# A two-layer decoder trunk on one core: key products among the index scores, all of the forgetting half ahead of the other half, and three weight splits moved from GpSimd to VectorE

## The chip, the core and the metric

The kernel runs on one core of a Trainium2 chip. The metric is the device time of one execution in microseconds (us). TensorE multiplies, VectorE (DVE in the rows), ScalarE (ACT) and GpSimd (POOL) do the elementwise work, SyncE (SP) and the other engines issue the DMAs. PEld is TensorE's weight load.

## The reference, cut to what matters

```
x: (1, 512, 1024) float32, two layers
even layer: h = x @ w_in, split into q_a, c_kv, q_idx, k_idx, w_idx, q_b, k_b, v_b, f_in
  index scores   score[t,s] = sum over 8 heads of w_idx[t,h] * relu(q_idx[t,h] . k_idx[s]), causal
  selection      the 128 best keys of each position
  8 heads "a"    softmax over the selected keys of (q_lat . c_kv + rel_bias), values c_kv
  8 heads "b"    forgetting heads: softmax of (q_b . k_b + cum_f[t] - cum_f[s]), values v_b
  m = concat(o_a, o_b) @ w_o
odd layer : gated projections and a short causal convolution, concat, @ w_o
each layer: x = LN(alpha*x + m); x = LN(alpha*x + conv_ffn(x)),  d_ff = 2816
```

## The kernel before, in words

All products are made at a precision near float32: every operand is cut into a high and a low part, and `mm3` (lines 179 to 183) or `mms` (line 185, the same as a generator that stops after each product) makes three products of 512 columns for one. The weights come as a stream of 128 x 1024 units (`Stream`). SyncE loads a unit into one of three `raw` buffers (line 62), ScalarE copies it to the high part (line 78), and the low part is a subtraction, on VectorE (line 82) or, for the units listed in `POOL_CUT`, on GpSimd (line 80). The parts lie in `whi`/`wlo` (three buffers each) or, for units named in `ws.big`, in one of 13 `quad` buffers. `unit()` hands out the next unit and splits two units ahead.

The order in which each engine takes its instructions is made when the kernel is built: a planner goes through the program, takes on each engine the earliest instruction of the program that its own time model holds to be ready, and lets later ones fill gaps. An engine then runs its list strictly in order. PSUM has eight banks; `bank()` takes one of the five of pool `ps5`, or, while `more` is not empty, in turn of eight also one of the three of pool `ps3`. Until the attention ends, the other three banks belong to `tri`, the tile into which `turn` transposes the soft-max weights.

The even layer goes in this order. (1) The first projections. (2) `pair_b(0)` makes the queries of forgetting heads 0 and 1, 24 products and a cut. (3) `scores(j)` for the three later blocks of 128 positions: for each of 8 heads two products into a bank (line 478), a ReLU on ScalarE (line 480), and a weighted sum into `sel[j]` on VectorE (lines 483 and 485). The first block needs no selection. (4) The rest of `pair_b(0)`: 24 key products. (5) Four value projections `proj_t` of 24 products, with the rounds of the selection `choose` (lines 497 and 499) on VectorE tied behind them in fixed portions by `step`. When a block's selection is done, GpSimd rescales it (line 503). (6) `pair_b(1)`, then the loop over head pairs by the string `SEQ`: `bias` on GpSimd, `logits` on TensorE, `soft` on VectorE and ScalarE (lines 667 and 669), `turn` (line 686), `values`, `divide`. Between these, `fill` takes products from `work()` (the projections of the later heads), and when these are gone from `begin()`, which is the first half (k = 0 to 3, the forgetting heads; units 23 to 26) of the attention's output projection. While `tri` lives, `begin()` opens three of its eight banks.

(7) `out_ln` adds the second half (k = 4 to 7, units 27 to 30, `us`) and normalises, in four chunks of 128 positions. With `begun` it takes on the remaining forgetting products bank by bank: ahead of chunk n those up to chunk n + 1. Behind each chunk stands `ln_chunk`: sums and statistics on VectorE (lines 261 to 269), a power on GpSimd (266), a scaling on ScalarE (272), an addition on GpSimd (273). `ln_turn` transposes the result on TensorE (284) and cuts it (`cut2`, lines 232 and 233). The next projection needs the turned chunks. The feed-forward layers and the odd layer call the same `out_ln` without `begun`: there a head part for all chunks comes first and 24 products for each chunk after it.

(8) Behind the first layer's feed-forward block the odd layer begins with four units of v, numbers 97 to 100 of the stream. Units 97 to 99 are the three that `POOL_CUT` names besides 12 to 22. Unit 105 gets a mask on GpSimd when it has been loaded (line 832).

Of the kernel before, what the change touches and what calls it, by code (L numbers as in the profile page):

```python
# [13 lines left out]
PSUM = bass.MemoryType.PSUM  # L14
# [4 lines left out]
NCH = 4  # L19
# [8 lines left out]
TAIL = 4  # L28
SEQ = "L0 4 S0 T0 B0 L1 4 S1 V1 3 L2 2 S2 T1 B1 R0 R1 4 V0 D 3"
GROUPS = ((3,), (2, 0), (1,))  # L30
POOL_CUT = tuple(range(12, 23)) + (97, 98, 99)
S1, S2, S3, S4 = 4, 3, 1, 2
WARM, WARM2 = 7, 5

# [62 lines left out]
def _body(ctx, tc, A):  # L97
# [9 lines left out]

    ps5 = E(tc.tile_pool(name="ps5", bufs=5, space=PSUM))
    ps3 = ExitStack()
    tri = ps3.enter_context(tc.tile_pool(name="tri", bufs=1, space=PSUM))  # L110
    more = []
    turnus = [0]

    def bank():
        turnus[0] += 1
        pool = more[0] if more and turnus[0] % 8 >= 5 else ps5
        return pool.tile([128, 512], F32, name="bank")

    def temp():
        return tmp.tile([128, 512], F32, name="temp")  # L120

    def quad(dt=FR):
        return quads.tile([128, 4, 512], dt, name="quad")

    ws = Stream(nc, A["ws"], rawp, wp, 2)
    ws.on_pool = POOL_CUT
    base = [0]

    def unit():
        i = base[0]  # L130
        base[0] += 1
        return ws.get(i)
# [46 lines left out]
    def mm3(out, a, b, first, last):  # L179

        nc.tensor.matmul(out, a[0], b[0], start=first, stop=False)  # L181
        nc.tensor.matmul(out, a[0], b[1], start=False, stop=False)  # L182
        return nc.tensor.matmul(out, a[1], b[0], start=False, stop=last)  # L183
# [18 lines left out]
    def wk(w, a, b):  # L202
        return w[0][:, a:b], w[1][:, a:b]
# [6 lines left out]
    def proj(w, xt):  # L210
        p = bank()
        half(w, xt, p, 0, S)
        return p
# [26 lines left out]
    def load_gb(l, i):  # L240
        q = quad(F32)
        for s, src in enumerate((A["ln_g"], A["ln_b"])):
            nc.gpsimd.dma_start(q[:, 2 * s:2 * s + 2].rearrange("p a b -> p (a b)"),
                                src[l, i].partition_broadcast(128))
        return [q[:, j] for j in range(4)]

    def load_res(src, n):
        r = []
        for hf in range(2):
            t = temp()  # L250
            nc.gpsimd.dma_start(t, src[n * 128:n * 128 + 128, hf * 512:hf * 512 + 512])  # L251
            r.append(t)
        return r

    def ln_chunk(n, ph, res, gb, dst):
        st = sm.tile([128, 2, 6], F32, name="st")
        mv = sm.tile([128, 2], F32, name="mv")
        ve = sm.tile([128, 1], F32, name="ve")
        rs = sm.tile([128, 1], F32, name="rs")
        for hf in range(2):  # L260
            nc.vector.scalar_tensor_tensor(out=res[hf], in0=res[hf], scalar=ALPHA, in1=ph[hf],
                                           op0=ALU.mult, op1=ALU.add)
            nc.vector.bn_stats(st[:, hf], res[hf])
        nc.vector.bn_aggr(mv, st)
        nc.vector.tensor_scalar(ve, mv[:, 1:2], EPS, None, op0=ALU.add)
        nc.gpsimd.tensor_tensor(out=rs, in0=ve, in1=mhalf, op=ALU.pow)
        for hf in range(2):
            r = res[hf]
            nc.vector.scalar_tensor_tensor(out=r, in0=r, scalar=mv[:, 0:1], in1=gb[hf],  # L269
                                           op0=ALU.subtract, op1=ALU.mult)  # L270
            if n < NCH - 1:
                nc.scalar.mul(r, r, rs)
                nc.gpsimd.tensor_tensor(out=r, in0=r, in1=gb[2 + hf], op=ALU.add)
            else:
                nc.vector.scalar_tensor_tensor(out=r, in0=r, scalar=rs, in1=gb[2 + hf],  # L275
                                               op0=ALU.mult, op1=ALU.add)
            nc.sync.dma_start(dst[n * 128:n * 128 + 128, hf * 512:hf * 512 + 512], r)

    def ln_turn(n, res, xt, after):
        for hf in range(2):  # L280
            r = res[hf]
            p = bank()
            for j in range(4):
                t = nc.tensor.transpose(p[:, j * 128:j * 128 + 128], r[:, j * 128:j * 128 + 128], ident)
                if j == 0 and after is not None:
                    tc.add_manual_dep(t.ins, after.ins.name, AFTER, reason="behind the products that hide the norm")
            c = slice(n * 128, n * 128 + 128)
            cut2(xt[0][hf][:, :, c], xt[1][hf][:, :, c], p.rearrange("p (a b) -> p a b", a=4))

    def out_ln(lhs, nk, res_src, l, i, dst, nbig, last=False, begun=None):  # L290

        head = nk - TAIL
        if begun is None:
            pb = [[None, None] for _ in range(NCH)]
            for hf in range(2):
                for n in range(NCH):
                    pb[n][hf] = bank()
            for k in range(head, nk + (0 if last else nbig)):
                ws.big[base[0] + k] = quad

            for k in range(head):
                w = unit()
                for hf in range(2):
                    for n in range(NCH):
                        mm3(pb[n][hf], lhs(k, n), wk(w, hf * 512, hf * 512 + 512), k == 0, False)
        else:
            pb, run = begun
        us = [unit() for _ in range(TAIL)]
        gb = load_gb(l, i)
        xt = None if last else [[quad(), quad()], [quad(), quad()]]  # L310
        rs = []
        for n in range(NCH):
            rs.append(load_res(res_src, n))
            while begun is not None and pb[min(n + 1, NCH - 1)][1] is None and next(run, "end") != "end":
                pass
            for hf in range(2):
                for k in range(head, nk):
                    m = mm3(pb[n][hf], lhs(k, n), wk(us[k - head], hf * 512, hf * 512 + 512),
                            k == 0, k == nk - 1)
                if not last and hf == 0 and n >= 2:  # L320
                    ln_turn(n - 2, rs[n - 2], xt, m)
            ln_chunk(n, pb[n], rs[n], gb, dst)
            if not last:
                ws.ready(base[0] + n + 1)
        late = None if last else [lambda m, n=n: ln_turn(n, rs[n], xt, m) for n in (2, 3)]
        return xt, late
# [54 lines left out]
    with ExitStack() as m0:  # L381
# [90 lines left out]
        def scores(j):  # L472
            n = 128 * (j + 1)
            for h in range(NH):
                c = slice(j * 128, j * 128 + 128)
                p = bank()
                for s in range(2):
                    nc.tensor.matmul(p[:, :n], qi[h % 2][:, h // 2, c], misc[:, s, :n], start=s == 0, stop=s == 1)
                t = temp()
                nc.scalar.activation(t[:, :n], p[:, :n], AF.Relu)  # L480
                s = wi[:, j, h:h + 1]
                if h == 0:
                    nc.vector.tensor_scalar(sel[j], t[:, :n], s, None, op0=ALU.mult)
                else:
                    nc.vector.scalar_tensor_tensor(out=sel[j], in0=t[:, :n], scalar=s, in1=sel[j],
                                                   op0=ALU.mult, op1=ALU.add)
            nc.gpsimd.affine_select(out=sel[j][:, n - 128:], in_=sel[j][:, n - 128:], pattern=[[-1, 128]],
                                    compare_op=ALU.is_ge, fill=-3e38, base=0, channel_multiplier=1)
# [25 lines left out]
        def pair_b(i):  # L514
            q = made[i] = quad()
            if i >= 1:
                ws.big[base[0] + 3] = quad
            for s, scale in ((0, -float(HD ** -0.5)), (2, 1.0)):
                w = unit()
                p = bank()  # L520
                for _ in proj_steps(w, xq, p):
                    yield
                cut2(q[:, s], q[:, s + 1], p, scale)
                if i < 2:
                    step(S2)
                yield
            finished.add(i)

        pair0 = pair_b(0)
        for _ in range(25):  # L530
            next(pair0)
        for j in (1, 2, 3):
            scores(j)
# [97 lines left out]
        def bias(h):  # L631
            if h < 16:
                biases[h] = (bias_b if h < 8 else bias_a)(h % 8)
# [113 lines left out]
        def lhs(k, n):  # L747
            c = slice(n * 128, n * 128 + 128)
            return oq[k // 2][:, k % 2, c], oq[k // 2][:, 2 + k % 2, c]

        pb = [[None, None] for _ in range(NCH)]
# [13 lines left out]
        begun = begin()  # L765
# [7 lines left out]
        def fill(n):  # L773
            for _ in range(n):
                next(todo, None)

        bias(0)
        bias(1)
        for i in range(10):
# [40 lines left out]
    with ExitStack() as m1:  # L820
# [59 lines left out]
        for i in range(4):  # L880
# [15 lines left out]
            pb = proj(unit(), xt)  # L896
# [97 lines left out]
```

## Time and profile before

| | |
|---|---|
| median of 3 runs | 1188.36 us (1187.03 to 1191.15) |
| the profiled execution's own time | 1188.65 us |
| its span, first to last instruction | 1186.9 us |
| mean granted TensorE clock | 0.992 of full speed |

The profile is of one execution. Its span is 1.75 us shorter than its own time; the execution lies 0.29 us above the median. A granted clock of 1.00 is 2.4 GHz, 0.50 is 1.2 GHz.

### The profile page before, as it was taken

What the parts mean: (1) busy time and instruction counts of PE and PEld (TensorE: products, weight loads), DVE (VectorE), ACT (ScalarE), POOL (GpSimd) and SP (SyncE); (2) the same over time, 40 slices, a digit from 0 to 9 for tenths busy, and PEclk for the clock granted to TensorE, in tenths of its full rate; (3) what the DMA queues carried; (4) which work ended last, traced back from release to release, by engine and by line L of the source; (5) the groups of instructions that cost most, each with busy time, mean ns of one, the idle gap of its engine ahead of it and who ended that gap; (6) DMA issues with size and microseconds to landing.
All of it is one profiled execution on the core that took longest, in us unless ns stands there. A gap on an engine that the chain in (4) does not pass through costs nothing. (4 is left out here: it accounts for less than half of the span.)

```text
span 1186.9 us, 14468 instructions
## 1 busy us (share of the span) xinstructions
PE 1157.8 (98%) x5532; PEld 960.0 (81%) x5532; DVE 692.9 (58%) x1134; ACT 464.0 (39%) x701; POOL 193.0 (16%) x251
## 2 busy tenths in 40 slices
PE   9899999899999999999999899999999999999997
PEld 7687877778888888888887688888888888888885
DVE  6788886557655666552227754456655666552226
ACT  7515657533444443432133232332444443432121
POOL 1218647214000000010014300003000000010003
PEclk9999999899999999999999899999999999999999
DMA  7522213343232323343245123371232323344221
GB/s 253 189 71 86 76 37 89 97 162 125 72 107 89 107 89 101 112 142 107 90 167 169 46 90 129 125 241 74 71 106 90 104 92 96 117 143 142 89 89 71
DMA packets 42261, 132.03 MB, mean 111 GB/s; under 512 B 5560, under 2 KB 6656, under 8 KB 42192
## 3 DMA queue, kind: packets, MB, share of 16 engines
q1 hardware_dynamic: 37280, 116.41, 29.9%
q0 software_dynamic: 4784, 14.67, 3.8%
q8 instruction: 43, 0.70, 0.3%
q14 instruction: 26, 0.21, 0.1%
q10 hardware_dynamic: 128, 0.03, 0.0%
HBM read 122.63 MB, written 10.02 MB: 112 GB/s over the span
## 5 line engine op out<-in xcount | busy, mean ns | idle before, releaser
L82 DVE TENSOR_TENSOR wlo<-raw,whi 128x1024 fp32r<-128x1024 f32 x150 | 186.1, 1242 | 281.4 <-ACT whi L78 281.2
L181 PE MATMUL bank<-quad,whi 128*128 128x512 f32 (+2 forms) x860 | 325.3, 379 | 1.4 <-ACT whi L146 0.8
L183 PE MATMUL bank<-quad,wlo 128*128 128x512 f32 (+2 forms) x860 | 325.4, 378 | 0.0
L182 PE MATMUL bank<-quad,whi 128*128 128x512 f32 (+2 forms) x860 | 325.4, 378 | 0.0
L78 ACT CAST whi<-raw 128x1024 fp32r<-128x1024 f32 x158 | 166.3, 1053 | 263.0 <-PE bank L183 119.8
L181 PEld LDWEIGHTS bank<-quad,whi 128*128 128x128 f32 x860 | 161.5, 188 | 31.5 <-ACT whi L146 1.3
L183 PEld LDWEIGHTS bank<-quad,wlo 128*128 128x128 f32 x860 | 161.7, 188 | 29.6
L182 PEld LDWEIGHTS bank<-quad,whi 128*128 128x128 f32 x860 | 161.8, 188 | 29.4 <-DVE quad L154 0.2
L182 PE MATMUL bank<-wlo,quad 128*128 128x512 f32 x356 | 138.5, 389 | 0.0
L183 PE MATMUL bank<-whi,quad 128*128 128x512 f32 x356 | 138.3, 389 | 0.0
L181 PE MATMUL bank<-whi,quad 128*128 128x512 f32 x356 | 138.2, 389 | 0.0
L251 POOL DMA_DIRECT2D temp<-x x24 | 13.1, 548 | 569.6 <-ACT quadx L367 424.9
L181 PEld LDWEIGHTS bank<-whi,quad 128*128 128x128 f32 x356 | 66.8, 188 | 14.2 <-issue 0.4
L183 PEld LDWEIGHTS bank<-whi,quad 128*128 128x128 f32 x356 | 66.8, 188 | 14.0
L182 PEld LDWEIGHTS bank<-wlo,quad 128*128 128x128 f32 x356 | 66.8, 188 | 13.8
L182 PE MATMUL bank<-quad 128*128 128x512 f32 (+1 forms) x192 | 69.6, 363 | 1.6 <-DVE quad L233 1.6
L336 DVE SCALAR_TENSOR_TENSOR temp<-bank,fcw,temp 128x511 f32<-128x511 f32 x88 | 65.5, 744 | 9.1 <-ACT temp L335 9.1
L181 PE MATMUL bank<-quad 128*128 128x512 f32 (+1 forms) x192 | 68.3, 363 | 0.5 <-ACT quad L232 0.5
L183 PE MATMUL bank<-quad 128*128 128x512 f32 (+1 forms) x192 | 68.7, 359 | 0.0
L338 DVE SCALAR_TENSOR_TENSOR temp<-bank,fcw,temp 128x510 f32<-128x510 f32 x88 | 65.9, 748 | 3.0
L335 ACT ACTIVATE temp<-bank,fcw 128x512 f32<-128x512 f32 x88 | 60.0, 681 | 10.8 <-PE bank L183 10.8
L363 ACT ACTIVATE temp<-temp 128x512 f32<-128x512 f32 x44 | 27.8, 632 | 88.7 <-DVE temp L338 88.7
(163 smaller groups left out, 1461.2 us busy)
## 6 DMA issues: line engine op xcount, KB each, us to landing
raw<-in_ws_dram SPq DMA_DIRECT2D x190, 512.0 KB, 3.5
x<-temp SPq DMA_DIRECT2D x24, 256.0 KB, 2.0
temp<-x POOLq DMA_DIRECT2D x24, 256.0 KB, 3.2
temp<-in_xT_dram SPq DMA_DIRECT2D x8, 256.0 KB, 7.0
temp<-fk_d SPq DMA_DIRECT2D x8, 256.0 KB, 5.4
temp<-rd_d SPq DMA_DIRECT2D x16, 128.0 KB, 3.0
temp<-in_x_dram POOLq DMA_DIRECT2D x8, 256.0 KB, 3.4
quad<-in_ln_g_dram POOLq DMA_DIRECT2D x4, 512.0 KB, 6.1
```

The lines of the kernel that those rows point to most:

```text
L78: nc.scalar.copy(hi, t)
L82: dve[0] = nc.vector.tensor_tensor(out=lo, in0=t, in1=_f(hi), op=ALU.subtract)
L181: nc.tensor.matmul(out, a[0], b[0], start=first, stop=False)
L182: nc.tensor.matmul(out, a[0], b[1], start=False, stop=False)
L183: return nc.tensor.matmul(out, a[1], b[0], start=False, stop=last)
L251: nc.gpsimd.dma_start(t, src[n * 128:n * 128 + 128, hf * 512:hf * 512 + 512])
L335: nc.scalar.mul(t, p, cw[:, j, 2:3])
L336: nc.vector.scalar_tensor_tensor(out=t[:, 1:], in0=p[:, :S - 1], scalar=cw[:, j, 1:2], in1=t[:, 1:], op0=ALU.mult, op1=ALU.add)
L338: nc.vector.scalar_tensor_tensor(out=t[:, 2:], in0=p[:, :S - 2], scalar=cw[:, j, 0:1], in1=t[:, 2:], op0=ALU.mult, op1=ALU.add)
L363: nc.scalar.activation(tg, tg, AF.Silu)
```

## The change

Three places move. The index scores get all eight banks: pool `ps3` is open from the start, and is closed for `tri` just ahead of the loop over head pairs. With each head of the scores one more step of `pair_b(0)` is taken, so that its 24 key products stand in the program among the 24 heads' score products; `unit()` for the key weights is called ahead of the scores. `out_ln` runs `begun` to its end before it calls for its own units and starts chunk 0. `POOL_CUT` no longer names units 97 to 99, whose subtraction is then made at line 82.

```diff
-POOL_CUT = tuple(range(12, 23)) + (97, 98, 99)
+POOL_CUT = range(12, 23)
@@ the PSUM pools
-    tri = ps3.enter_context(tc.tile_pool(name="tri", bufs=1, space=PSUM))
-    more = []
+    more = [ps3.enter_context(tc.tile_pool(name="ps3", bufs=3, space=PSUM))]
@@ out_ln
             pb, run = begun
+            for _ in run:
+                pass
         us = [unit() for _ in range(TAIL)]
...
             rs.append(load_res(res_src, n))
-            while begun is not None and pb[min(n + 1, NCH - 1)][1] is None and next(run, "end") != "end":
-                pass
@@ scores
             for h in range(NH):
+                next(pair0, None)
                 c = slice(j * 128, j * 128 + 128)
                 p = bank()
@@ ahead of the loop over head pairs
+        ps3.close()
+        more.clear()
+        tri = ps3.enter_context(tc.tile_pool(name="tri", bufs=1, space=PSUM))
         bias(0)
         bias(1)
```

## Rows read from the trace of the kernel before

**Rows 1.** The page of the profiled execution, its first line and the busy time of the engines (busy us, share of the span, instructions).

```profile
span 1186.9 us, 14468 instructions
...
PE 1157.8 (98%) x5532; PEld 960.0 (81%) x5532; DVE 692.9 (58%) x1134; ACT 464.0 (39%) x701; POOL 193.0 (16%) x251
```

**Rows 2.** The waits of TensorE over the whole span, longest in total first: tile and line that waited, who ended the wait, us in total, times, longest.

```profile
PE bank L478 <- ACT temp L480: 5.4, 4, 1.9
PE bank L284 <- POOL temp L273: 4.9, 2, 3.8
PE bank L188 <- ACT pt L232: 3.8, 3, 3.2
```

**Rows 3.** Busy time in chosen stretches: stretch, its length, then busy us (and instructions) of PE, PEld, DVE, ACT and POOL, the granted TensorE clock as a share of full speed, the DMA share and GB/s.

```profile
43.10:59.10 16.00, 10.13 (x49) 7.28 (x48) 14.58 (x19) 13.13 (x27) 5.80 (x3) 1.00 0.49 166
59.10:200.00 140.90, 140.60 (x746) 111.21 (x747) 114.75 (x300) 74.64 (x163) 78.02 (x124) 1.00 0.22 70
...
214.80:220.00 5.20, 5.18 (x16) 3.94 (x17) 4.06 (x10) 3.74 (x13) 1.19 (x1) 0.50 0.87 253
256.00:300.00 44.00, 42.19 (x264) 37.55 (x263) 28.19 (x46) 11.14 (x17) 15.18 (x11) 1.00 0.34 113
...
656.50:664.00 7.50, 6.45 (x20) 5.15 (x21) 5.70 (x27) 1.17 (x2) 3.84 (x3) 0.54 0.37 142
780.00:840.00 60.00, 59.76 (x363) 53.14 (x363) 36.01 (x56) 18.93 (x26) 11.56 (x10) 1.00 0.36 127
```

**Rows 4.** The timeline of TensorE around the index scores (start us, length us, instruction, how many; in brackets the idle time before and what ended it). L478 is a score product, the L188 of 59.10 the first key product, the L181 of 64.59 the first value product.

```profile
43.12 1.11 PE L478 MATMUL bank<-quad 128*128 128x256 f32 x8
...
47.09 3.18 PE L478 MATMUL bank<-quad 128*128 128x256 f32 x18 [1.88 <-ACT temp L480]
...
56.92 2.35 PE L478 MATMUL bank<-quad 128*128 128x512 f32 x8 [1.67 <-ACT temp L480]
59.10 0.64 PE L188 MATMUL bank<-quad,whi 128*128 128x512 f32 x2
...
64.59 0.39 PE L181 MATMUL bank<-quad 128*128 128x512 f32 x1
```

**Rows 5.** The timelines of VectorE and of GpSimd from the scores to the first soft-max.

```profile
44.89 3.50 DVE L82 TENSOR_TENSOR quad<-raw,quad 128x1024 fp32r<-128x1024 f32 x3 [0.24 <-ACT quad L78]
...
66.13 0.69 DVE L233 TENSOR_TENSOR quad<-bank,quad 128x512 fp32r<-128x512 f32 x1
...
70.85 0.69 DVE L233 TENSOR_TENSOR quad<-bank,quad 128x512 fp32r<-128x512 f32 x1 [1.20 <-ACT quad L232]
...
87.17 0.69 DVE L233 TENSOR_TENSOR quad<-bank,quad 128x512 fp32r<-128x512 f32 x1 [0.94 <-ACT quad L232]
...
100.58 0.56 DVE L667 CUSTOM_DVE_ANT_0 d<-bank,d 128x384 f32<-128x384 f32 x1
...
90.09 0.41 POOL L503 TENSOR_SCALAR sel<-sel 128x256 f32<-128x256 f32 x1 [21.25 <-DVE sel L502]
```

**Rows 6.** The groups of TensorE between 216 and 253.1 us and then between 253.1 and 279.5 us (line, operation, tile, count, busy us and mean ns): L188 with whi or wlo is a product of the forgetting half, L181 to L183 are products of the other half.

```profile
L188 PE MATMUL bank<-whi,quad 128*128 128x512 f32 x24 | 9.7, 455 | 0.0
...
L181 PE MATMUL bank<-quad 128*128 128x512 f32 x12 | 4.4, 392 | 0.0
...
L188 PE MATMUL bank<-whi,quad 128*128 128x512 f32 x24 | 8.1, 390 | 0.0
...
L181 PE MATMUL bank<-quad 128*128 128x512 f32 x20 | 7.7, 394 | 0.0
```

**Rows 7.** The norm behind the attention's output projection: timelines of TensorE, VectorE and GpSimd.

```profile
281.50 0.39 PE L182 MATMUL bank<-quad 128*128 128x256 f32 x1 [1.57 <-DVE quad L233]
...
260.90 1.29 DVE L261 SCALAR_TENSOR_TENSOR temp<-temp,bank 128x512 f32<-128x512 f32 x2 [4.57 <-PE bank L183]
...
268.81 5.69 DVE L82 TENSOR_TENSOR wlo<-raw,whi 128x1024 fp32r<-128x1024 f32 x3
...
280.78 0.67 DVE L233 TENSOR_TENSOR quad<-bank,quad 128x512 fp32r<-128x512 f32 x1
...
268.77 8.13 POOL L273 TENSOR_TENSOR temp<-temp,quad 128x512 f32<-128x512 f32 x4
...
280.24 2.52 POOL L273 TENSOR_TENSOR temp<-temp,quad 128x512 f32<-128x512 f32 x2 [0.83 <-ACT temp L272]
```

**Rows 8.** The norm between the two layers: timelines of VectorE, GpSimd and SyncE.

```profile
629.11 1.23 DVE L82 TENSOR_TENSOR wlo<-raw,whi 128x1024 fp32r<-128x1024 f32 x1 [13.35 <-ACT whi L78]
...
645.36 2.99 DVE L82 TENSOR_TENSOR quad<-raw,quad 128x1024 fp32r<-128x1024 f32 x1 [0.47 <-ACT quad L78]
...
641.94 2.96 POOL L273 TENSOR_TENSOR temp<-temp,quad 128x512 f32<-128x512 f32 x2 [1.54 <-ACT temp L272]
644.87 2.40 POOL L80 TENSOR_TENSOR quad<-raw,quad 128x1024 fp32r<-128x1024 f32 x1
...
652.04 1.10 POOL L832 TENSOR_SCALAR_AFFINE_SELECT raw<-raw 128x1024 f32<-128x1024 f32 x1 [0.65 <-DMA raw<-in_ws_dram]
...
654.77 3.37 POOL L273 TENSOR_TENSOR temp<-temp,quad 128x512 f32<-128x512 f32 x2
...
648.38 0.81 SPq L62 DMA_DIRECT2D raw<-in_ws_dram  x2
```

**Rows 9.** The subtractions of a split on VectorE that write a quad: count, shortest, median and longest ns.

```profile
L82 DVE TENSOR_TENSOR quad<-raw,quad x26: 1210/1225/2993, 34.2 to 1148.6; 128x1024 fp32r<-128x1024 f32 x26
```

## The prediction

> **What bounds the kernel now.** I read the page first: TensorE is busy for 1157.8 of 1186.9 us and the next engine, VectorE, for 58% of the span [rows 1]. Only what TensorE stands idle, or runs at the low clock, can be won or lost, so the second view is its waits. Three names lead: score products that wait for a ReLU, 5.4 us; transposes of a norm that wait for GpSimd's addition, 4.9 us; attention products that wait for a cut on ScalarE, 3.8 us [rows 2]. The third view, busy time by stretch, puts them in their places and gives the clock beside them [rows 3]. From 43.1 to 59.1 us TensorE works 10.13 of 16.00 us, at clock 1.00. From 59.1 to 200 us it stands 0.3 us. Behind the stall that ends at 214.8 us the clock is 0.50 for 5.2 us; behind the one that ends at 656.5 us it is 0.54 for 7.5 us. The timelines then say what each stall waits for [rows 4, 5, 7, 8].
>
> **The scores and the key products.** Every head of the scores needs a bank, and gets it when a ReLU has read it. With five banks the PE queue stops for up to 1.88 us at a time, and the last score products end where the first key product starts, at 59.10 us; the value products begin at 64.59 us [rows 4]. So 24 key products take 64.59 − 59.10 = 5.49 us, 0.229 us each. They have no input of the scores. Put among the heads, they find 5.87 us of idle time (16.00 − 10.13 [rows 3]) and fit. If the last score product stays where it is, the value products start 5.5 us earlier. Three more banks, less the one that the keys hold, can bring the last score forward too. The most that can be won is all that the stage takes beyond its work. The first eight score products, 256 columns wide, take 1.11 us, 0.14 us each [rows 4]; 512 columns take 0.229 us, and 384 some 0.18 us, the mean of both. With 16 of each width that is 8.8 us of work, so the upper bound is 16.0 − 8.8 = 7.2 us.
>
> Does the gain last? VectorE is the slower engine here: its weighted sums follow three subtractions that start at 44.89 us and end ahead of the key cut at 66.13 us, and nothing of the change shortens that. After it come cuts and selection rounds. In the four value projections VectorE waits for TensorE each time, 1.20 us at the first cut and 0.94 us at the last of four, 4.0 us in all (1.20 + 0.93 + 0.94 + 0.94) [rows 5]. If TensorE comes early, these waits go, and the first selection ends 4.0 us earlier. That matters because GpSimd's rescaling at 90.09 us waited 21.25 us for it, and the first forgetting bias is queued behind it. So 4.0 us is sure to pass on to the attention loop. TensorE gets by until then with its own projections, and VectorE's further waits up to the first soft-max at 100.58 us can give the other 1.5 us. I take **−5.5 us**, bounds −7.2 and, if VectorE or the planner's order lets none of it through, 0. The clock did not fall in this stretch, so there is nothing to win by it. The key weights' earlier `unit()` call costs nothing: it asks for one more split ahead of the scores, and three splits stand there already, at 44.89 us. Closing the pool for `tri` costs nothing either while the first `turn` lies a whole pair behind; without that cover it would be one cut, 0.69 us.
>
> **Three units back on VectorE.** This takes three subtractions of about 2.4 us off GpSimd and puts three of 1.225 us (the median [rows 9]) on VectorE. Units 97 and 98 are split before 629.11 us, where VectorE had stood for 13.35 us [rows 8]: no cost. Unit 99 is split at 644.87 us on GpSimd, in the middle of the norm. The subtraction of unit 100 on VectorE, from 645.36 to 648.35 us, took 2.99 us instead of 1.225 and ended 1.08 us behind GpSimd's, which ran to 647.27 us. On VectorE alone the two are 2.45 us and end at about 647.3 us, 1.0 us earlier. What hangs on it: the next loads are issued at 648.38 us, as that buffer comes free; the mask at 652.04 us waits for such a load; chunk 2's addition starts only behind it, at 654.77 us [rows 8], and the transposes behind that. So the stall of 3.8 us becomes 2.8 us: **−1.0 us**. Stalls of 1.9 us left the clock at 1.00 in the scores, and the one of 3.2 us did not [rows 2, 3]; 2.8 us lies between, nearer to the second, so I let the clock fall as before. Bounds: −8.3 us, if the whole stall goes (4.9 us of waits) and with it the low clock (7.5 × (1 − 0.54) = 3.45 us); and +1.2 us if the added subtraction falls beside GpSimd's two additions of chunk 1, which start at 641.94 us and take 1.48 us each: then its 1.225 us stands in the norm's own chain and nothing is saved.
>
> That pair of rows shows a subtraction on VectorE which waits for one on GpSimd. The Trainium skill (SBUF — State Buffer, Who interferes with whom) has the rule: a VectorE instruction with two inputs in SBUF and a GpSimd instruction that reads SBUF lock each other out, and the later one stands until the first is done. By that rule the trace agrees at 645.36 us, and it speaks against this edit at every other place: each subtraction that comes to VectorE can now be held by an addition of the norm, or hold it.
>
> **All of the forgetting half first.** Of the 96 forgetting products, 48 are done by 253.1 us and 48 after it; of the other half 36 are done before and 60 after (24 + 24 with a high or low part of three kinds, 12 and 20 rows for each of three products [rows 6]). Before, half of the late 48 stood behind chunk 0's last products. Now all stand ahead, so chunk 0's norm, whose first sum began at 260.90 us, begins 24 × 0.229 = 5.5 us later, at 266.4 us. From 260.90 us to the cut that released TensorE, 281.45 us, VectorE works almost without a pause: 20.55 us, of which three splits in a row take 5.69 us instead of 3 × 1.225 = 3.7, beside four additions on GpSimd of 2.03 us each instead of 1.26 [rows 7]. These splits waited for buffers that late forgetting products still read. Now those products end sooner, and the splits can go into the idle 4.57 us ahead of the first sum. Then the norm needs 20.55 − 5.69 = 14.86 us and ends at 281.3 us: the same stall as before, 1.57 us. If half of the 3.7 us of splits still falls between the sums, it is worse by 1.2 to 1.8 us. The odd layer's norm has the new order already, head part first and 24 products a chunk, and TensorE stands 0.24 us in 60 there [rows 3]. I take **+0.6 us**, bounds −1.8 (all 1.81 us of idle time from 256 to 300 us gone [rows 3]) and +8.95 (no split goes ahead: 5.5 us more stall and 3.45 us of low clock).
>
> **Sum.** 1188.65 − 5.5 − 1.0 + 0.6 = 1182.75 us on the profiled execution's time, which lies 0.3 us above the median: 1182.5 us. Against 1188.36 us, 0.3% is 3.6 us, about what a measurement here can tell from no change.
>
> **The rivals.** *The boundary clears* as well: 7.3 us more than I take, 1175 us. For it speaks that GpSimd is empty at 643 us; against it, that mask and DMA issues still stand ahead of the addition. *VectorE or the planner keeps the scores' gain*: the selection is not earlier, or the key products are not taken in the gaps; then 1188.65 − 1.0 + 0.6 = 1188.3, some 1188 us. For it speaks VectorE at 114.75 of 140.9 us after the scores [rows 3]; against it, its waits for TensorE. *The norm is late in full*: 8.35 us more than I take, 1191 us; against it stands the odd layer. *The added subtraction is held up* beside chunk 1's additions: 2.2 us more than I take, 1184.7 us, at the edge of no change; against it, those additions are over at 644.90 us, when unit 99 was cut before. This is what the Trainium skill's rule on the shared SBUF port (SBUF — State Buffer) would do here.
>
> *Slower*: the fill goes. In 216 to 253.1 us, between transposes and values, TensorE did 36 products of the other half, 36 × 0.229 = 8.2 us [rows 6]. They now stand in the program behind forgetting products whose banks come free only when `tri` is given back. If the planner no longer takes them early, the gaps are idle: +8.2 us, and a fall of the clock with 2.6 us (5.2 × 0.50 [rows 3]), 1193.3 us. It decides from about 26 of the 36 products on, where 5.9 us are eaten. Against it: before, they also had forgetting products without a bank ahead of them, and ran.
>
> **How the numbers follow.** Forecast, 1179 to 1184.7 us: 0.47. Boundary clears: 0.12. Gain kept by VectorE or planner: 0.18. Norm late: 0.08. Held up: 0.05, of which 0.03 counts as faster and 0.02 as the same. Fill gone: 0.10. So faster 0.62, same 0.28, slower 0.10. The range goes from the cleared boundary, 1175 us, to the late norm, 1191 us, and leaves out the fill and what lies under 1175.
>
> **What would show it.** Right: between 43 and 60 us key products lie among score products, TensorE has under 1 us of waits for a ReLU, and the first value product starts at 58 to 60 us; the first soft-max moves by 4 to 6 us; no subtraction of some 2.4 us on GpSimd near 645 us and none of 3 us on VectorE; the transposes of chunk 2 wait 2 to 3 us. Wrong: the first soft-max still near 100 us, a wait over 3 us ahead of the first feed-forward products, or idle time between 216 and 253 us in place of the other half's products.

## The result, and the profile after

The changed kernel takes 1178.14 us, the median of five executions (1176.54 to 1181.81), against 1188.36 us: a ratio of 0.9917, 95% interval 0.9894 to 0.9941, 10.2 us less. Forecast were 1182.5 us, with 1175 to 1191 as the range. It is faster by 0.8%, more than the 0.3% that can be told, and 4.4 us below the forecast: inside the range, but 0.9 us under the 1179 to 1184.7 us that the prediction gave to its own forecast. The profiled execution took 1180.2 us and is one of the two slower ones of five; their mean granted clocks are 0.993 and 0.992, those of the others 0.996 to 0.997. One place where it lost clock is seen below.

The page, the waits of TensorE and stretches of its busy time, all of the changed kernel. Its line numbers lie one lower than before up to about L474 (L181 is now L180, L284 is L283) and three higher at the end (the mask's L832 is L835).

```profile
PE 1156.4 (98%) x5532; PEld 960.3 (81%) x5532; DVE 699.4 (59%) x1137; ACT 463.8 (39%) x701; POOL 183.6 (16%) x248
```

```profile
PE bank L187 <- ACT pt L231: 3.7, 3, 3.2
PE bank L181 <- DVE quad L232: 3.2, 1, 3.2
...
PE bank L283 <- POOL temp L272: 0.9, 2, 0.6
PE bank L181 <- DVE quad L82: 0.8, 2, 0.6
PE bank L478 <- ACT temp L480: 0.8, 2, 0.4
```

```profile
43.10:58.20 15.10, 14.33 (x73) 11.90 (x72) 13.19 (x16) 13.17 (x26) 6.29 (x4) 1.00 0.57 182
...
256.00:300.00 44.00, 40.58 (x256) 37.10 (x255) 31.82 (x48) 12.84 (x20) 13.62 (x10) 0.92 0.26 84
276.30:284.00 7.70, 7.61 (x43) 7.61 (x44) 7.19 (x13) 1.33 (x2) 4.90 (x4) 0.63 0.19 72
656.00:664.00 8.00, 8.00 (x41) 6.72 (x40) 6.70 (x35) 1.56 (x3) 1.66 (x1) 1.00 0.18 70
```

Of the three waits that led [rows 2], the one for a ReLU fell from 5.4 to 0.8 us and the one for GpSimd's addition from 4.9 to 0.9 us; the one for the cut of `pt` is as it was. A new one stands second: products of the feed-forward block wait 3.18 us in one piece for a cut on VectorE, where they had waited 1.57 us [rows 7], and behind it the clock is 0.63 for 7.7 us.

**The scores.** The timeline of TensorE: L187 is a key product, L478 a score product, the L180 at 58.23 us the first value product.

```profile
43.19 0.40 PE L478 MATMUL bank<-quad 128*128 128x256 f32 x2
43.42 0.40 PE L187 MATMUL bank<-quad,whi 128*128 128x512 f32 x1
...
50.14 2.86 PE L478 MATMUL bank<-quad 128*128 128x384 f32 x16
...
56.27 2.12 PE L478 MATMUL bank<-quad 128*128 128x512 f32 x8 [0.35 <-ACT temp L480]
58.23 0.39 PE L180 MATMUL bank<-quad 128*128 128x512 f32 x1
```

Key and score products alternate from 43.19 us; the last key product ends at about 50.3 us, and the values begin at 58.23 instead of 64.59 us [rows 4]. Further on, VectorE's first soft-max and GpSimd's rescaling, to be set beside [rows 5]:

```profile
95.18 0.54 DVE L667 CUSTOM_DVE_ANT_0 d<-bank,d 128x384 f32<-128x384 f32 x1
...
86.53 0.41 POOL L503 TENSOR_SCALAR sel<-sel 128x256 f32<-128x256 f32 x1 [15.08 <-DVE sel L502]
```

The rescaling comes 3.6 us earlier and the soft-max 5.4 us. VectorE's four waits for TensorE between the cuts [rows 5] are gone.

**The norm behind the attention's output projection.** VectorE and TensorE:

```profile
255.53 1.37 DVE L260 SCALAR_TENSOR_TENSOR temp<-temp,bank 128x512 f32<-128x512 f32 x2 [5.98 <-PE bank L182]
...
264.73 4.54 DVE L82 TENSOR_TENSOR wlo<-raw,whi 128x1024 fp32r<-128x1024 f32 x2
...
269.78 1.71 DVE L82 TENSOR_TENSOR wlo<-raw,whi 128x1024 fp32r<-128x1024 f32 x1
...
276.39 0.58 PE L181 MATMUL bank<-quad 128*128 128x256 f32 x1 [3.18 <-DVE quad L232]
```

The three splits still stand between the sums, 6.25 us of them (they were 5.69 us [rows 7]). What the front of the kernel had won, 5.1 us by 276.39 us (it was 281.50 [rows 7]), is 2.7 us when the next stage, whose transposes began at 293.74 us before, begins at 291.08 us.

**The norm between the layers.** Before, GpSimd's power for chunk 2 came at 650.40 us, as VectorE's statistics were ready:

```profile
650.40 0.99 POOL L266 TENSOR_TENSOR rs<-ve,mhalf 128x1 f32<-128x1 f32 x1 [3.13 <-DVE ve L265]
```

In the changed kernel, VectorE and GpSimd:

```profile
642.49 2.46 DVE L268 SCALAR_TENSOR_TENSOR temp<-temp,mv,quad 128x512 f32<-128x512 f32 x2
...
646.67 4.13 DVE L82 TENSOR_TENSOR quad<-raw,quad 128x1024 fp32r<-128x1024 f32 x2
...
644.37 1.00 POOL L265 TENSOR_TENSOR rs<-ve,mhalf 128x1 f32<-128x1 f32 x1
646.20 1.30 POOL L272 TENSOR_TENSOR temp<-temp,quad 128x512 f32<-128x512 f32 x1 [0.83 <-ACT temp L271]
...
653.74 1.10 POOL L835 TENSOR_SCALAR_AFFINE_SELECT raw<-raw 128x1024 f32<-128x1024 f32 x1 [2.99 <-DMA x<-temp]
```

The orders on both engines are others than before [rows 8]. On VectorE chunk 2's statistics precede the splits of units 99 and 100, so that its power comes at 644.37 us. On GpSimd chunk 2's two additions (646.20 and 648.06 us) precede the mask, which had stood between power and additions. Beside these additions the two splits take 4.13 us instead of 2.45, and TensorE waits 0.8 us for them. It waits nowhere longer than 0.6 us there, and the clock is 1.00. The odd layer's table load on ScalarE comes at 828.62 instead of 837.03 us, 8.4 us earlier: 5.7 of these were won at this boundary, 2.7 before it.

### The profile page after: what moved, and what is told of

It reads as the page before. It is cut to its first block, busy times and chain, and to the rows that moved or that the text cites. A ratio compares the mean times of both kernels' runs of the same rounds, so it can differ in the third digit from the quotient of the medians.

```text
span 1178.5 us, 14462 instructions
## 1 busy us (share of the span) xinstructions
PE 1156.4 (98%) x5532; PEld 960.3 (81%) x5532; DVE 699.4 (59%) x1137; ACT 463.8 (39%) x701; POOL 183.6 (16%) x248
## 5 line engine op out<-in xcount | busy, mean ns | idle before, releaser
L180 PE MATMUL bank<-quad,whi 128*128 128x512 f32 (+2 forms) x860 | 325.2, 379 | 1.4 <-ACT whi L145 1.4
L181 PE MATMUL bank<-quad,whi 128*128 128x512 f32 (+2 forms) x860 | 325.3, 378 | 0.0
L182 PE MATMUL bank<-quad,wlo 128*128 128x512 f32 (+2 forms) x860 | 325.2, 378 | 0.0
L180 PEld LDWEIGHTS bank<-quad,whi 128*128 128x128 f32 x860 | 161.5, 188 | 30.7 <-ACT whi L145 1.8
L181 PEld LDWEIGHTS bank<-quad,whi 128*128 128x128 f32 x860 | 161.7, 188 | 29.8
L182 PEld LDWEIGHTS bank<-quad,wlo 128*128 128x128 f32 x860 | 161.7, 188 | 29.6
L181 PE MATMUL bank<-wlo,quad 128*128 128x512 f32 x356 | 138.5, 389 | 0.0
L182 PE MATMUL bank<-whi,quad 128*128 128x512 f32 x356 | 138.3, 389 | 0.0
L180 PE MATMUL bank<-whi,quad 128*128 128x512 f32 x356 | 138.2, 389 | 0.0
L180 PEld LDWEIGHTS bank<-whi,quad 128*128 128x128 f32 x356 | 66.8, 188 | 14.4 <-issue 0.4
L181 PEld LDWEIGHTS bank<-wlo,quad 128*128 128x128 f32 x356 | 66.8, 188 | 13.9
L182 PEld LDWEIGHTS bank<-whi,quad 128*128 128x128 f32 x356 | 66.8, 188 | 13.7
L181 PE MATMUL bank<-quad 128*128 128x512 f32 (+1 forms) x192 | 70.0, 366 | 4.0 <-DVE quad L232 3.2
L182 PE MATMUL bank<-quad 128*128 128x512 f32 (+1 forms) x192 | 69.3, 362 | 0.0
L180 PE MATMUL bank<-quad 128*128 128x512 f32 (+1 forms) x192 | 68.6, 363 | 0.5 <-ACT quad L231 0.5
```

## The experiments

None of these kernels leaves out any part of the reference. "Before" is the kernel before, measured beside each of them; a ratio is given with its 95% interval.

**Each part alone.** `only_scores` is the kernel before with the eight banks and the interleaved key products, `only_cut` with the new `POOL_CUT`, `only_forget` with the new order in `out_ln`; `no_forget` is the changed kernel with the old order in `out_ln`. The diff of each is that part of the change.

> The kernel before with the eight banks and the key products among the scores, nothing else. Theory (the three edits act each at its own place): value products start near 58.2 us, some 6.4 us earlier than in the kernel before, and of this 5.5 to 6.5 us reach the end: 1182 to 1183 us; the stalls at both norms stay as they were (1.6 us and 3.8 us). Rival (the score edit gives little by itself and the boundary between the layers gives most): within 3 us of the kernel before.

> The kernel before with units 97 to 99 split on VectorE, nothing else. Theory (GpSimd's subtraction held VectorE's in the middle of the norm between the layers): the 3.8 us wait for GpSimd's addition goes below 1.5 us and the clock stays at 1.00 behind it, 5 to 8 us earlier: 1180 to 1183 us. Rival (the stall went because the other edits changed the order of the instructions): the wait stays over 3 us and the time within 2 us of the kernel before.

> The kernel before with all of the forgetting half ahead of the other half, nothing else. Theory (this edit alone makes the longer stall at the attention's norm): the wait for the cut of the norm grows from 1.6 to about 3.2 us, 1.5 us slower where the clock stays and up to 4 us slower where it falls: 1189 to 1192 us. Rival (the longer stall comes from another edit): the wait stays at 1.6 us and the time within 1 us.

> The changed kernel with the old order in the output projection, so with the score edit and the three units on VectorE alone. Theory: the stall at the attention's norm is 1.6 us again and the clock does not fall there, 1.5 to 4 us faster than the changed kernel: 1174.5 to 1176.5 us. Rival (the order matters for later places, the boundary among them): the boundary's stall is back, 1182 us or more.

| kernel | median, us | before, us | ratio |
|---|---|---|---|
| scores alone | 1182.05 | 1187.48 | 0.9953 [0.9939, 0.9967] |
| `POOL_CUT` alone | 1180.76 | 1187.48 | 0.9945 [0.9932, 0.9957] |
| forgetting alone | 1189.80 | 1187.48 | 1.0021 [1.0012, 1.0031] |
| changed kernel without forgetting | 1174.89 | 1187.48 | 0.9893 [0.9879, 0.9906] |

Each of the four times lies in the range of its theory; that the subtraction on GpSimd is the reason in `only_cut`, as its theory has it, does not hold (below). The scores give −5.4 us, the three units −6.7 us, the forgetting half costs 2.3 us. The sum is −9.8 us, and 10.2 were measured: the parts hardly touch one another. Without its third part the changed kernel is faster by another 2.9 us (0.0024 of 1188 us by the two ratios; 3.2 us by the medians); its slowest execution, 1175.97 us, is below the fastest of the changed kernel, 1176.54. The norm of `no_forget`, on VectorE and TensorE, and behind it the stretch of the norm in `only_forget`:

```profile
254.63 1.28 DVE L260 SCALAR_TENSOR_TENSOR temp<-temp,bank 128x512 f32<-128x512 f32 x2 [3.28 <-PE bank L182]
...
262.53 5.69 DVE L82 TENSOR_TENSOR wlo<-raw,whi 128x1024 fp32r<-128x1024 f32 x3
...
275.23 0.39 PE L181 MATMUL bank<-quad 128*128 128x256 f32 x1 [1.57 <-DVE quad L232]
```

```profile
256.00:300.00 44.00, 40.58 (x241) 35.50 (x239) 31.25 (x47) 12.45 (x19) 15.84 (x14) 1.00 0.39 131
```

The wait is 1.57 us here, as before, and 3.18 us with the third part; `only_forget` alone has 3.19 us. Behind that the clock stays at 1.00 in `only_forget`, where the changed kernel, with the same 40.58 us of work in the 44 us, had 0.92. Chunk 0's first sum is not 5.5 us earlier without that part but 0.90 us (254.63 against 255.53). The splits stand between the sums in both.

**Banks without keys, keys without banks.** `only_banks` is the scores' part without its line in the head loop, `only_keys` is that line alone.

```diff
             for h in range(NH):
+                next(pair0, None)
```

> The kernel before with eight banks for the scores, the key products still behind all of them. Theory (the idle time is filled by the key products; banks only move the wait): the score stage is bound by ReLUs and weighted sums, its last product moves by no more than 1 to 2 us, 1186 to 1187.5 us. Rival (the banks alone do it, since TensorE no longer waits for a ReLU): value products start near 59 us, 1182 to 1183 us.

> The kernel before with the key products among the scores and five banks, of which the keys hold one. Theory: the 5.5 us of key products still fit the idle time, which is bound by ReLUs; value products start at 59 to 60.5 us, 1182 to 1184 us. Rival (four banks for the scores hold up the last score products as much as the keys gain): value products start after 62 us, 1185 us or more.

Measured: 1184.87 us with ratio 0.9991 [0.9981, 1.0001] for the banks, 1185.88 us with 0.9995 [0.9985, 1.0005] for the keys. Neither gains anything that can be told (2.0 and 0.9 us by the medians, and both intervals hold 1), and together they gave 0.9953. The banks' time lies between those of theory and rival, the keys' where the rival had it. TensorE in `only_banks` (L187 is a key product, L477 a score product, L180 at 64.37 us the first value product), then in `only_keys` (L479 a score product, L181 at 63.10 us the first value product). The profiled execution of `only_banks` is the slowest of its twelve, 1189.82 us, and its clock was 0.83 from 43.1 to 59.1 us and 0.90 from there to 66 us; so its 24 key products take 7.0 us instead of 5.5.

```profile
56.66 0.90 PE L477 MATMUL bank<-quad 128*128 128x512 f32 x2 [1.78 <-ACT temp L479]
57.36 1.16 PE L187 MATMUL bank<-quad,whi 128*128 128x512 f32 x2
...
64.37 0.39 PE L180 MATMUL bank<-quad 128*128 128x512 f32 x1
```

```profile
53.78 5.51 PE L479 MATMUL bank<-quad 128*128 128x384 f32 x24 [1.32 <-DVE quad L233]
61.42 1.88 PE L479 MATMUL bank<-quad 128*128 128x512 f32 x4 [2.12 <-ACT temp L481]
63.10 0.69 PE L181 MATMUL bank<-quad 128*128 128x512 f32 x1
```

With eight banks the last score product ends only 1.7 us earlier (57.36 against 59.10 us [rows 4]): the ReLUs set the pace, the last of 24 starts at 60.1 us against 60.4 us. The ReLUs in turn wait 2.02 us for a weighted sum on VectorE, in both kernels. With keys alone TensorE takes most of the keys in one piece ahead of the score products. The ReLUs start as early, at 46.4 us, but the last one only at 64.7 us, and five banks make the last score products wait for them: the values begin at 63.10 us, at less than the full clock (0.75 from 59.1 to 66 us). With both parts the last ReLU is late too, at 63.6 us. But now eight banks hold the scores that are still to be read, so the values start at 58.23 us, 5.4 us ahead of it.

**Which of the three units.** Both kernels are the kernel before with a shorter list: in `pool99` only unit 99 stays on GpSimd, in `pool9798` units 97 and 98.

```diff
-POOL_CUT = tuple(range(12, 23)) + (97, 98, 99)
+POOL_CUT = tuple(range(12, 23)) + (99,)
...
+POOL_CUT = tuple(range(12, 23)) + (97, 98)
```

> The kernel before with units 97 and 98 on VectorE and unit 99 alone left on GpSimd. Theory (only unit 99's subtraction lies in the norm, and it is what held VectorE's for 2.99 us): the 3.8 us wait is there as before, 1187 to 1189 us. Rival (the two early units decide, by what they do to the loads and to the order of the later splits): the wait is gone, 1180 to 1182 us.

> The kernel before with unit 99 on VectorE and units 97 and 98 left on GpSimd. Theory: the wait is gone as with all three moved, 1180 to 1182 us. Rival (the early units decide): the 3.8 us wait is there, 1186 us or more.

Measured: with unit 99 left on GpSimd 1180.24 us against 1186.82, ratio 0.9946 [0.9931, 0.9960], the whole gain of `only_cut`. With 97 and 98 left there 1188.38 us, ratio 1.0011 [1.0001, 1.0021], no gain, and a wait of 5.07 us. In both the rival was right. VectorE and GpSimd in the first:

```profile
648.46 2.15 DVE L82 TENSOR_TENSOR quad<-raw,quad 128x1024 fp32r<-128x1024 f32 x1
...
646.15 1.00 POOL L266 TENSOR_TENSOR rs<-ve,mhalf 128x1 f32<-128x1 f32 x1
647.12 2.40 POOL L80 TENSOR_TENSOR quad<-raw,quad 128x1024 fp32r<-128x1024 f32 x1
649.48 2.28 POOL L273 TENSOR_TENSOR temp<-temp,quad 128x512 f32<-128x512 f32 x1
...
654.64 1.11 POOL L832 TENSOR_SCALAR_AFFINE_SELECT raw<-raw 128x1024 f32<-128x1024 f32 x1
```

and in the second:

```profile
642.50 2.36 DVE L82 TENSOR_TENSOR quad<-raw,quad 128x1024 fp32r<-128x1024 f32 x2
...
648.41 0.16 DVE L265 TENSOR_SCALAR ve<-mv 128x1 f32<-128x1 f32 x1
...
648.74 1.45 POOL L832 TENSOR_SCALAR_AFFINE_SELECT raw<-raw 128x1024 f32<-128x1024 f32 x1 [6.13 <-DMA raw<-in_ws_dram]
...
651.83 1.68 POOL L266 TENSOR_TENSOR rs<-ve,mhalf 128x1 f32<-128x1 f32 x2
653.69 3.39 POOL L273 TENSOR_TENSOR temp<-temp,quad 128x512 f32<-128x512 f32 x2 [0.19 <-ACT temp L272]
```

In the first, VectorE's subtraction lies beside GpSimd's and takes 2.15 us instead of 1.225 [rows 9], and nothing is lost: the additions go first and the mask behind them. In the second, nothing contends (two subtractions in 2.36 us), and GpSimd stands 6.13 us at the mask, for a load, with chunk 2's power and additions queued behind it. Most of these 6.13 us cost nothing, since chunk 2's statistics end only at 648.57 us (L265); the power, which could start then, starts at 651.83 us. So the overlap of two subtractions does not set the stall. The orders do, and two of them differ: the mask on GpSimd, ahead of chunk 2's additions or behind them, and the splits on VectorE, ahead of chunk 2's statistics or behind them.

**The order by itself.** `mask_late` is the kernel before, units 97 to 99 on GpSimd as they were, with unit 105's mask tied behind chunk 2's last addition.

```diff
-                nc.gpsimd.tensor_tensor(out=r, in0=r, in1=gb[2 + hf], op=ALU.add)
+                last_add[0] = nc.gpsimd.tensor_tensor(out=r, in0=r, in1=gb[2 + hf], op=ALU.add)
...
-            nc.gpsimd.affine_select(out=t, ...
+            m = nc.gpsimd.affine_select(out=t, ...
+            tc.add_manual_dep(m.ins, last_add[0].ins.name, AFTER, ...)
```

> The kernel before, all three units on GpSimd as there, with one tie more: the mask of unit 105 on GpSimd goes behind the last addition of the norm's third chunk. Theory (the early units decide because with them the planner put the mask, which waits for a load, ahead of chunk 2's addition on GpSimd): the 3.8 us wait falls to 1 to 2 us, the clock stays at 1.00, 1181 to 1184 us. Rival (VectorE is the one that is late, by the splits of units 99 and 100 ahead of chunk 2's statistics): the wait stays over 3 us and the clock falls, 1186 us or more.

Measured: 1183.36 us against 1188.02, ratio 0.9958 [0.9946, 0.9971]. VectorE, GpSimd and TensorE:

```profile
645.71 2.99 DVE L82 TENSOR_TENSOR quad<-raw,quad 128x1024 fp32r<-128x1024 f32 x1 [0.47 <-ACT quad L78]
...
653.37 2.51 POOL L274 TENSOR_TENSOR temp<-temp,quad 128x512 f32<-128x512 f32 x2
655.81 1.11 POOL L833 TENSOR_SCALAR_AFFINE_SELECT raw<-raw 128x1024 f32<-128x1024 f32 x1
...
654.71 0.65 PE L285 MATMUL bank<-ident,temp 128*128 128x128 f32 x4 [1.66 <-POOL temp L274]
```

The theory was right: the mask's place alone is worth 4.7 us, where `only_cut` gave 6.7. The stall of 3.84 us becomes 1.66, and behind it the clock stays at 1.00. The subtraction of 2.99 us is as long as before, and it still precedes chunk 2's statistics, which in `only_cut` and `pool99` go first. What is left, 2 us, fits that order on VectorE (2.2 us of waits for GpSimd's additions remain here, none in `only_cut`), but that is not shown: the intervals of the two ratios overlap, and the order on VectorE was not tried by itself.

**A version that beats both.** `late_copies` is `no_forget` with two of the `hi` copies that stand ahead of the cut of `pt` put behind it. The edit has two parts, which were not tried apart: a tie for the copies of units 27 and 28, and `ws.ahead = 0`, by which `begin()` no longer splits two units ahead. In `no_forget` ScalarE copies three weight blocks from 204.36 to 207.30 us and cuts `pt` at 208.09 us, for which TensorE waits 3.13 us, the wait that is in all kernels so far.

```diff
-        nc.scalar.copy(hi, t)
+        m = nc.scalar.copy(hi, t)
+        if i in (27, 28):
+            self.tie(m)
...
+            if h == 13:
+                a13 = act[0]
+                ws.tie = lambda m: tc.add_manual_dep(m.ins, a13.ins.name, AFTER, ...)
...
+            ws.ahead = 0
             us = [unit() for _ in range(4)]
+            ws.ahead = 2
```

> The changed kernel with the old order in the output projection (the fastest so far, 1174.9 us), and the copies of units 27 and 28 on ScalarE tied behind the cut of turn 13, for which TensorE waits 3.1 us near 209 us. Theory (three copies of 0.98 us stand ahead of that cut): two go, the wait falls to about 1.2 us and the clock stays at 1.00 behind it, 2.0 + 2.6 us less: 1170 to 1171.5 us. Rival (the cut also waits for the soft-max's exponentials, or the products that use units 27 and 28 come too late and leave gaps): 1174 us or more.

Measured: 1171.51 us against 1188.02, ratio 0.9855 [0.9840, 0.9870], which is 3.4 us by the medians and 4.5 by the ratios under `no_forget`, and under the changed kernel 6.6 and 7.4. ScalarE and TensorE (L79 is a `hi` copy, L234 the cut of `pt`, L190 the product that waits for it), then two stretches of `late_copies` and the first of them in `no_forget`:

```profile
203.96 1.05 ACT L79 CAST quad<-raw 128x1024 fp32r<-128x1024 f32 x1
...
205.80 1.21 ACT L234 CAST pt<-tri 128x1280 fp32r<-128x1280 f32 x1
...
207.06 0.56 PE L190 MATMUL bank<-pt,quad 128*128 128x512 f32 x2 [1.27 <-ACT pt L234]
...
190.00:225.00 35.00, 33.06 (x203) 27.09 (x202) 20.78 (x52) 23.26 (x55) 14.68 (x25) 0.95 0.20 65
...
256.00:300.00 44.00, 43.76 (x298) 40.11 (x297) 31.17 (x45) 18.75 (x27) 12.90 (x9) 1.00 0.27 96
```

```profile
190.00:225.00 35.00, 31.67 (x189) 26.04 (x189) 22.54 (x55) 23.40 (x54) 16.80 (x24) 0.95 0.30 92
```

One copy is left ahead of the cut, and the wait is 1.27 us, as the theory had it. The clock did not stay at 1.00, as it should have: behind a wait of 1.27 us it falls as far as behind one of 3.13, to 0.95 on the mean of 190 to 225 us in both kernels. So nothing came of the 2.6 us for the clock. The time reached the edge of the theory's range by something not aimed at: the norm, too, no longer waits (43.76 of 44.00 us busy, against 42.19 in `no_forget` as in the kernel before [rows 3]). Why it doesn't was not tried.

## Why the prediction was right or wrong

**Scores, −5.5 forecast, −5.4 measured.** The size and the place came as worked out: the values at 58.23 us, where 58 to 60 was named, waits for a ReLU 0.8 us, the first soft-max 5.4 us earlier. VectorE's waits for TensorE gave the 4 us that were called sure, seen as 3.6 us at the rescaling. One step beneath it was wrong: the text let the keys fill the idle time "if the last score product stays where it is" and gave the three banks a bonus beyond that. With five banks the last score product does not stay; the score products end at 63.10 us instead of 59.10, and the keys alone gain nothing that can be told. Banks and keys are one measure.

**Three units, −1.0 forecast, −6.7 measured.** This term was mis-sized, and it is most of the 4.4 us by which the forecast was too high. The step that failed is "Units 97 and 98 are split before 629.11 us ...: no cost". What they cost is no time of their own. With them on GpSimd, that engine's order has the mask, and the load that it waits for, ahead of chunk 2's additions, and VectorE's order has a split ahead of chunk 2's statistics; with them on VectorE both are turned round. `pool99` and `pool9798` show that this pair decides, and `mask_late` that the mask's place is worth 4.7 us. Unit 99, on which the −1.0 us was built, brings nothing by itself: `pool9798` has it on VectorE and is no faster. The text had seen the mask in the chain, but took the order on the queue as fixed and moved only the time of its load. The rival that the boundary clears, −8.3 us there, was given 0.12, and it is what came at that place. Its reason was not the right one: it went by an empty GpSimd at 643 us, and `pool99` clears the boundary with a subtraction on GpSimd at 647.12 us. What spoke against it, the mask ahead of the addition, is what moved. Why the planner puts the mask elsewhere when two earlier subtractions change engine was not tried.

The Trainium skill's rule on the shared port (SBUF — State Buffer, Who interferes with whom) agrees with the rows where two subtractions overlap, 2.99 and 2.15 us instead of 1.225. The rival "held up" occurred in small: the two splits that take 4.13 us instead of 2.45 do so beside chunk 2's additions, not chunk 1's, and TensorE waits 0.8 us for them, where the rival had 2.2.

**Forgetting, +0.6 forecast, +2.3 measured alone and +2.9 in the changed kernel.** The sign was right, and the value lies inside the bounds of −1.8 and +8.95. Two of its steps failed. Chunk 0's first sum is not 5.5 us late but 0.9: the order in the program is not TensorE's. Of the 24 forgetting products that `no_forget` has behind chunk 0's products, the changed kernel still has the last 12 there, from 260.54 us on. So the last of them does not end sooner, as the text had it, but at 263.4 us against 262.8. And the splits did not move into the idle time ahead of the first sum; all 6.25 us stay between the sums. In the forecast these two shifts, 5.5 us later and 5.69 us less, cancelled one another and left 0.6 us; neither came, and that the sign was right is luck in part. The wait grew from 1.57 to 3.18 us, 1.6 us: the first sum is 0.90 us later, the way from there to the cut takes 20.86 us instead of 20.60, and TensorE has run out of work 0.45 us sooner (273.21 against 273.66 us). In the profiled execution the clock behind it cost 7.7 × (1 − 0.63) = 2.8 us more. The two together are 4.4 us. Over five executions the part costs 2.9, so not every execution can have lost that clock, and the profiled one of `only_forget` kept it behind the same wait. That the two slower ones of the five are those that lost it is argued from their mean clocks; only one of the five has a trace.

**The slower rival**, that the fill goes, did not occur. Between transposes and values 36 products of the other half still stand in the gaps (209 to 246 us, 12 each from L180, L181 and L182), as before [rows 6], and the two waits in that stretch, 3.5 us for the cut of `pt` on ScalarE and 1.0 for that on VectorE, were there before.

**The sum.** With the sizes measured alone it is 1188.36 − 5.4 − 6.7 + 2.3 = 1178.6 us, 0.4 us above the median that came. The forecast, 1182.5, is 4.4 us higher: the three units gave 5.7 us more than it took, and the forgetting cost 1.7 us more. That the time lies so near is luck in part: the two errors go against one another, and the range was 16 us wide. Of the signs named beforehand, one for wrong came, a wait over 3 us ahead of the first feed-forward products (3.18 us), and one for right did not, the wait of 2 to 3 us at chunk 2's transposes, which don't wait at all.

## What to carry to other kernels

A wait of an engine that works in order is to be priced with what is queued behind it: here a mask that waited for its load held a norm's addition, and tying the mask behind the addition was worth 4.7 us without moving any work. Where a change moves work off an engine, ask what order that engine has afterwards, not only when it ends. Fill for idle slots and the buffers that let the slots run ahead are worth trying together: each alone gave nothing here that could be told, both gave 5.4 us.

## What was not expected of the hardware

The prediction took the clock at the scores as 1.00, from the one execution of before [rows 3]. Kernels whose scores were left as they were fell there in some executions. The stretch from 43.1 to 59.1 us and the next in `pool99`:

```profile
43.10:59.10 16.00, 11.13 (x46) 8.91 (x46) 14.52 (x18) 13.18 (x27) 5.85 (x3) 0.83 0.48 165
59.10:66.00 6.90, 6.90 (x29) 5.69 (x28) 6.48 (x11) 2.18 (x5) 0.75 (x1) 0.90 0.00 0
```

The values begin at 66.07 us there, 1.5 us later than in before, behind stalls of up to 1.9 us, as there. `only_forget` and `mask_late` fall there too (0.89 and 0.85), `only_cut` and `pool9798` show 1.00. In the four profiled kernels with both parts of the scores it is 1.00 every time. The length of a stall does not sort the other places either: 3.18 us in the changed kernel took the clock down and 3.19 us in `only_forget` did not, and 1.27 us in `late_copies` took it down as far as 3.13 us in `no_forget`. The prediction had sorted them so, a stall of 2.8 us as "nearer to the second"; the runs do not bear that out. So stalls of nearly equal length leave the clock up in one execution and take it down in another, and a profile of one execution does not tell what a stall costs on the mean.
